# Building a neighbourhood bias in single transfers across the first feed-forward block

## Chip, cores and metric

One core of a Trainium2 chip. The time is device microseconds of one execution; three runs of the kernel before are known.

## What is computed

The reference is a small transformer trunk in float32 on 256 tokens (a grid of 4 rows by 64 columns) and 16 meta tokens, width 1024. Layer 0 mixes tokens by neighbourhood attention, layer 1 by differential attention, and each layer has a SwiGLU feed-forward block (FFN, hidden width 2816) before and after the mixing:

```python
for i in range(DEPTH):                                     # DEPTH = 2
    g = norm_g[i]
    f1 = swiglu(rmsnorm(h, g[0]), ffn_w_gate[i, 0], ffn_w_up[i, 0], ffn_w_down[i, 0])
    h = h + FFN_RES * rmsnorm(f1, g[1])
    hn = rmsnorm(h, g[2])
    if i % N_MIXERS == 0:
        m = neighborhood_attention(hn, ..., na_rpb[j], na_meta_bias[j])
    else:
        m = diff_attention(hn, ..., t5_rel_bias, lambda_init)
    h = h + rmsnorm(m, g[3])
    f2 = swiglu(rmsnorm(h, g[4]), ffn_w_gate[i, 1], ffn_w_up[i, 1], ffn_w_down[i, 1])
    h = h + FFN_RES * rmsnorm(f2, g[5])
```

In the neighbourhood attention each of 16 heads adds to a logit a learned bias that depends on the offset between query and key (`rpb`, 16 x 15 x 31), and a query sees only 16 columns of keys. The change is about how that bias, with the mask of the columns, is put together on the chip.

## The kernel before

**Weights.** All weights stream from DRAM as 328 units of 128 x 8 x 128 floats (512 KB) in the order of their use. `load` (line 110) issues one transfer from SyncE (SP) into one of 5 `raw` buffers. ScalarE writes the rounded half `whi` (line 126, `split_hi`) and VectorE the rest `wlo` (line 132, `split_lo`), two operations each, into one of 7 split slots (`W_BUFS`). A product is three matmuls, `mm3` (lines 179 to 181): whi with the data's high part, wlo with the high part, whi with the low part. A unit has 24 of them. The end of a unit's split frees its raw buffer, and `split_lo` then issues the next load; so the load of unit i + 5 stands on SP behind the split of unit i. A split needs a free slot, that is the last product of the unit seven before.

**The first FFN** (`ffn`, line 420). Its up part has 22 steps f. A step is two units (gate and up, 48 matmuls), then `evac(f)`: VectorE scales both sums (lines 436, 437), ScalarE takes the Silu, and VectorE multiplies and stores the result in two parts. Inside `evac` two further units are split. Steps 0 to 2 are set up by `start`; from f=3 on, one function of the list `extra` is called after each `evac`. Then come the down products, 22 units in 8 output tiles m, with a split per unit (`pump`) for 16 of 22 positions and `post.feed` after each tile.

**The bias** (`natten_bias`, line 559) is that list `extra`. In order: `small_loads`, `begin`, nothing, four `expand`, nothing, eight `mask`; 16 steps, so f=3 to f=18. `begin` loads the mask (128 x 2 x 160) and issues four transfers DRAM to DRAM, which cut the padded table `rpbP` into four copies `tab`, in pieces of 4 floats (line 570). `expand(rq)` issues two transfers that spread table rq over 32 partitions, 16 heads by 160 floats each (line 579). `mask` adds the mask to 4 heads at once (line 586), and POOL copies the meta bias in (line 590). All transfers are issued by SP, in program order, on one queue; SP waits at a load until the split that frees its buffer is done, and what is behind waits too.

**Order.** Within an engine the order is that of the code. PE's order is written out by hand (`manual_schedule`). The bias is first read by the neighbourhood attention (line 746).

Of the kernel before, what the change touches and what calls it, by code (L numbers as in the profile page):

```python
# [17 lines left out]
P = 128  # L18
# [8 lines left out]
ROWS = 4  # L27
# [20 lines left out]
def encoder_kernel(ctx, tc, xT, wall, gT, bqkvT, boT, sublnT, rpbP, metab, lam_p, rel,  # L48
# [23 lines left out]
    def acc_tile():  # L72
        """a bank for sums; outside attention its banks are taken too"""
        pools["turn"] = (pools["turn"] + 1) % 7
        if pools["wide"] and pools["turn"] % 2:
            return att_tile()
        return psum.tile([P, 512], F32, tag="acc", name=nm("acc"), bufs=4)
# [6 lines left out]

# [1 line left out]
    h = state.tile([P, KB, T], F32, tag="h", name="h")  # L86
# [14 lines left out]

# [1 line left out]
    # the split of unit i takes the slot of unit i - W_BUFS, so it comes after that one's  # L103
    # last product in the engines' order
    raw = {}
# [33 lines left out]
    def split_part(k, nk):  # L139
        """parts of the first units' splits"""  # L140
        for ahead in range(FIRST):
            split_hi(k, nk, ahead)
        for ahead in range(FIRST):
            split_lo(k, nk, ahead if k + nk < KB else 0)

    def pump_hi():
        """the first half of a split's work, if there is a slot; pump_lo does the rest"""
        i = count["split"]
        pending[0] = i < UNITS and i - W_BUFS < count["done"]
        if pending[0]:  # L150
            split_hi(0)
            split_hi(KB // 2)
# [30 lines left out]
    def proj(acc, n, ihi, ilo, hook=None):  # L183
        """products of one unit"""
        w = next_unit()
        for k in range(KB):
            if hook is not None and k in hook:
                hook[k]()
            mm3(acc[:, :n], w[0][:, k, :], w[1][:, k, :], ihi[:, k, :n], ilo[:, k, :n], k == 0, k == KB - 1)
        done()  # L190

    def proj_group(units, n_of, ihi, ilo, accs, hook):
        """k-outer products of several units, each into its own bank"""
        ws = [next_unit() for _ in units]
# [11 lines left out]

# [1 line left out]
    first = [load((2, 2, 4)) for _ in range(FIRST)]  # L208
# [23 lines left out]

# [1 line left out]
    def chunks(n):  # L234
        """first tokens of chunks of 128 that cover n tokens"""
        return (0, P, T - P) if n == T else (0, P)

    def sums_of(st, col, sq, n):
        """sums over the partitions of sq, with tokens on partitions"""
        cs = chunks(n)  # L240
        for i, c in enumerate(cs):
            nc.tensor.matmul(st[:, col + i:col + i + 1], sq[:, c:c + P], ones, start=True, stop=True)
        return st[:, col:col + len(cs)]
# [16 lines left out]
    def spread(st, r, n):  # L260
        """the tokens' values on all partitions, in PSUM"""
        for i, c in enumerate(chunks(n)):
# [20 lines left out]
    class InputRstd:  # L283
        """the token's 1/rms of h, computed between products"""

# [21 lines left out]
    class Post:  # L307
        """post-norm of one sub-layer, fed tile by tile: h grows by r * f with f the
        fed tiles times their gain and r the token's 1/rms"""

# [52 lines left out]
    def enter(post, n_of, ab, rest):  # L363
        """the first products of a sub-layer. Those of its first unit begin before the
        last post-norm is known: with h = h' + r f they are W h' + r (W f). Those of the
        units after it are k-outer, as h comes."""
        n0 = n_of(0)
# [28 lines left out]

# [1 line left out]
    def start(n):  # L398
        """the first products of all, as the data come"""
        gain = gains(0, 0)  # L400
# [19 lines left out]
    def ffn(l, which, n, before, gain_next, n_next, extra=()):  # L420
        extra = list(extra)
        with all_banks(), tc.manual_schedule():
# [6 lines left out]
            with tc.tile_pool(name=nm("ffn"), bufs=1) as fp:  # L429
# [17 lines left out]
                with tc.tile_pool(name=nm("fft"), bufs=2) as ft:  # L447
# [10 lines left out]
                    if which == 0:  # L458
                        nc.scalar.activation(warm, ones, AF.Exp)
                        if l == 1:  # L460
                            lambda_scalar()
                assert not extra
                if gain_next is None:
# [6 lines left out]
                for m in range(KB):  # L470
                    ps = acc_tile()
                    for f in range(FT):
                        idx = m * FT + f
                        if idx % KB == 0:
                            if w is not None:
                                done()
                            w = next_unit()
                            if idx % FT < 16:
                                pump(1)
# [3 lines left out]
                    if m < KB - 1:  # L483
                        for i in range(m + m // 6, m + 1 + (m + 1) // 6):
                            input_hi(i, gain_next, n_next)
                            input_lo(i, gain_next, n_next)
                done()
            return post

    def last_down(lp, mhi, mlo):  # L490
        """the last products, with tokens on partitions, and the last post-norm"""
        f = fg.rearrange("p a b -> p (a b)")[:, :2 * D].rearrange("p (t d) -> p t d", t=2)
# [18 lines left out]
        def finish(t, c):  # L511
            """statistics and gain of one piece"""
            at, n = pieces[t][c]
# [43 lines left out]

# [1 line left out]
    def natten_bias(holder):  # L559
        """steps that build the logit bias of the neighbourhood attention"""  # L560
        steps = []
        holder["tab"] = dram.tile([H0, ROWS, 79, ROWS], F32, tag="tab0", name="tab0")

        def begin():
            bt = biasp.tile([P, H0 * 2 * NK], F32, tag="bias", name="bias0")
            holder["b0"] = bt.rearrange("p (h q k) -> p h q k", h=H0, q=2)
            holder["wm"] = pools["tmp"].tile([P, 2, 160], F32, tag="wmask", name="wm", bufs=1)
            nc.sync.dma_start(holder["wm"], wmask)
            for rq in range(ROWS):
                nc.sync.dma_start(holder["tab"][:, rq, :, :], rpbP[:, :, 7 - rq:11 - rq])  # L570

        def expand(rq):
            def go():
                for qt in range(2):
                    src = holder["tab"][:, rq, :, :].rearrange("h x r -> h (x r)")
                    src = bass.AP(src.tensor, src.offset + (0 if qt == 0 else 32),
                                  [[4, 32], [ROWS * 79 * 4, H0], [1, 160]])
                    o = 0 if qt == 0 else NMETA
                    nc.sync.dma_start(holder["b0"][rq * 32:(rq + 1) * 32, :, qt, o:o + 160], src)
            return go  # L580

        def mask(qt, h0):
            def go():
                b4, wm = holder["b0"], holder["wm"]
                o = 0 if qt == 0 else NMETA
                nc.vector.tensor_tensor(out=b4[:, h0:h0 + 4, qt, o:o + 160], in0=b4[:, h0:h0 + 4, qt, o:o + 160],
                                        in1=wm[:, qt, :].unsqueeze(1).broadcast_to([P, 4, 160]), op=ALU.add)
                o = 160 if qt == 0 else 0
# [3 lines left out]

        return ([small_loads, begin, lambda: None] + [expand(r) for r in range(ROWS)] + [lambda: None]
                + [mask(qt, h0) for qt in range(2) for h0 in range(0, H0, 4)])

    tab1 = dram.tile([H1, T5N], F32, tag="tab1", name="tab1")

    def t5_bias(holder):
        """steps that build the relative-position bias of the differential attention"""
        nst = T5N // T5CH + 1  # L600
# [68 lines left out]
    def grid_rev(ap):  # L669
        """[p, (c r)] -> [p, q, c', r] with the columns from last to first"""  # L670
        return ap.rearrange("p (c r) -> p c r", r=ROWS)[:, ::-1, :].rearrange("p (q c) r -> p q c r", q=2)

    def q_order(ap):
        """[p, (q r c')] -> [p, q, c', r]"""
        return ap.rearrange("p (q r c) -> p q c r", q=2, r=ROWS)
# [4 lines left out]
    def token_order(ap):  # L680
        """[p, (q r c')], last tile first, -> [p, q, c, r]"""
        return ap[:, :NG].rearrange("p (q r c) -> p q c r", q=2, r=ROWS)[:, :, ::-1, :]

# [1 line left out]
    def natten(l, b4, before, gain_next, n_next):  # L685
        with ExitStack() as outer, ExitStack() as inner:
# [117 lines left out]

            # meta queries against meta keys, some pairs of heads at once
            meta = {}
# [64 lines left out]
    class Filler:  # L871
        """products that need no attention, to be set between its steps"""

# [34 lines left out]
    def pipeline(fl, steps, pumps, single=()):  # L908
        """attention of the pairs of heads, with products in between: a pair begins every
        8 chunks, and steps are (chunk from the pair's beginning, function of the pair)"""  # L910
        steps = sorted(steps, key=lambda t: -t[0])
# [31 lines left out]

# [1 line left out]
    def diff_attention(l, b4, before, gain_next, n_next):  # L945
# [139 lines left out]

# [1 line left out]

# [10 lines left out]
def _units(inputs):  # L1098
    """weights as [units, 128, 8, 128] in the order of their use"""
    def cols(w):  # L1100
# [28 lines left out]
def _t5_bucket(rel):  # L1129
    """bucket of a relative position: halves by sign, exact below 8, then by thresholds"""  # L1130
    n = np.abs(rel)
# [5 lines left out]
def _constants():  # L1137
# [7 lines left out]

    wm = np.zeros((P, 2, 160), np.float32)
    cq = np.arange(P) % 32
    kc = np.arange(160) // 4
    for qt, (c, k) in enumerate(((63 - cq, kc + 24), (31 - cq, kc))):
# [39 lines left out]
```

## Time and profile before

| | |
|---|---|
| Three runs | 1108.76, 1117.27, 1122.29 us (median 1117.27) |
| Span of the profiled execution | 1120.7 us (its time outside the span isn't given) |
| PE busy | 1093.9 us, 98% |
| VectorE (DVE) busy | 777.2 us, 69% |
| ScalarE (ACT) busy | 611.7 us, 55% |
| Weight loads | 326 of 512 KB, 3.9 us to landing (median) |
| Table transfers | 4 of 19.8 KB, 14.6 us to landing |
| Bias transfers | 8 of 320 KB, 19.2 us to landing |

A slice of the page is 1/40 of the span, 28 us. The shares are means over stages: what a stage costs is seen in windows of it and in the chain of waits, which follows the work that ended last back through what released it. Matmuls are pipelined: each is shown with 0.29 us, but they start 0.126 us apart.

### The profile page before, as it was taken

To read this page: it belongs to the slowest core of one execution; us is meant where nothing else is said; L and a number is where in the kernel's file an instruction comes from. 1 tells how busy PE (TensorE), PEld (TensorE's weight loads), DVE (VectorE), ACT (ScalarE), POOL (GpSimd) and SP (SyncE) were. 2 spreads that over 40 slices of the span, in tenths; PEclk is the share of its full clock that TensorE was granted. 3 is DMA by queue.
4 is the path that set the end of the run, shared out by engine and by line. 5 is a ranking of instruction groups with operands and counts; after the bars stand their busy time and mean duration, and the time that the engine had idled before them with its cause. 6 is when DMAs were issued, how large, how long until landed. Compare 5 with 4: busy or idle time off the path is not lost.

```text
span 1120.7 us, 22216 instructions
## 1 busy us (share of the span) xinstructions
PE 1093.9 (98%) x8492; PEld 1060.0 (95%) x8492; DVE 777.2 (69%) x1645; ACT 611.7 (55%) x1398; POOL 131.8 (12%) x234
## 2 busy tenths in 40 slices
PE   7988899999999999999999999999999999999997
PEld 7988899999989999999999999999989999999986
DVE  5745696578677796666568766566886778966643
ACT  4533456548667464445545544455577865655541
POOL 4000000043122300000011000001311222000000
PEclk9998999999999999999999999999999999999999
DMA  7569866525333275496534655465253242755551
GB/s 248 175 95 206 214 209 211 183 96 182 101 113 107 84 230 187 161 225 213 178 124 134 224 171 169 161 207 183 75 167 118 95 151 83 242 187 187 189 169 38
DMA packets 64955, 181.90 MB, mean 162 GB/s; under 512 B 13832, under 2 KB 22192, under 8 KB 64848
## 3 DMA queue, kind: packets, MB, share of 16 engines
q1 hardware_dynamic: 64848, 180.48, 53.4%
q8 instruction: 67, 1.10, 0.4%
q14 instruction: 40, 0.33, 0.1%
HBM read 179.33 MB, written 1.20 MB: 161 GB/s over the span
## 4 chain that ended last, share of the span: by engine, by line
PE 82%; DVE 8%; DMA 5%; issue 2%; ACT 2%; POOL 0%; SPq 0%; POOLq 0%; DVEq 0%; ACTq 0%
PE acc L179 14%; PE acc L181 14%; PE acc L180 14%; PE att L179 9%; PE att L181 8%; PE att L180 8%; DVE wlo L132 3%; DMA raw<-wall 3%; DMA bias<-tab 2%; DVE h L357 1%; DVE xlo L280 1%; ACT whi L126 1%; PE acc L200 1%; PE acc L204 1%; PE acc L509 1%
## 5 line engine op out<-in xcount | busy, mean ns | idle before, releaser
L132 DVE TENSOR_TENSOR wlo<-raw,whi 128x512 fp32r<-128x512 f32 (+1 forms) x660 | 438.5, 703 | 83.3 <-ACT whi L126 79.6
L126 ACT CAST whi<-raw 128x512 fp32r<-128x512 f32 (+1 forms) x660 | 374.1, 612 | 122.0 <-issue 43.3
L179 PE MATMUL acc<-xhi,whi 128*128 128x272 f32 (+1 forms) x1016 | 300.5, 296 | 5.6 <-ACT whi L126 5.6
L180 PE MATMUL acc<-xhi,wlo 128*128 128x272 f32 (+1 forms) x1016 | 292.8, 288 | 0.7 <-DVE wlo L132 0.7
L181 PE MATMUL acc<-xlo,whi 128*128 128x272 f32 (+1 forms) x1016 | 293.1, 288 | 0.0
L179 PEld LDWEIGHTS acc<-xhi,whi 128*128 128x128 f32 x1016 | 192.6, 190 | 11.7 <-ACT whi L126 6.0
L180 PEld LDWEIGHTS acc<-xhi,wlo 128*128 128x128 f32 x1016 | 192.8, 190 | 1.3 <-DVE wlo L132 1.3
L181 PEld LDWEIGHTS acc<-xlo,whi 128*128 128x128 f32 x1016 | 192.7, 190 | 0.0
L179 PE MATMUL att<-xhi,whi 128*128 128x272 f32 (+1 forms) x560 | 161.9, 289 | 4.6 <-ACT whi L126 4.6
L180 PE MATMUL att<-xhi,wlo 128*128 128x272 f32 (+1 forms) x560 | 161.3, 288 | 0.7 <-DVE wlo L132 0.7
L181 PE MATMUL att<-xlo,whi 128*128 128x272 f32 (+1 forms) x560 | 161.5, 288 | 0.0
L438 ACT ACTIVATE gt<-gt 128x272 f32<-128x272 f32 (+1 forms) x88 | 37.7, 428 | 152.7 <-DVE gt L436 152.7
L179 PEld LDWEIGHTS att<-xhi,whi 128*128 128x128 f32 x560 | 106.2, 190 | 5.7 <-ACT whi L126 5.0
L180 PEld LDWEIGHTS att<-xhi,wlo 128*128 128x128 f32 x560 | 106.1, 189 | 1.1 <-DVE wlo L132 1.1
L181 PEld LDWEIGHTS att<-xlo,whi 128*128 128x128 f32 x560 | 106.2, 190 | 0.0
L179 PE MATMUL acc<-mhi,whi 128*128 128x272 f32 x286 | 83.0, 290 | 0.0
L181 PE MATMUL acc<-mlo,whi 128*128 128x272 f32 x286 | 82.5, 289 | 0.0
L180 PE MATMUL acc<-mhi,wlo 128*128 128x272 f32 x286 | 82.4, 288 | 0.0
L273 POOL TENSOR_TENSOR sqa<-sqa,sq 128x272 f32<-128x272 f32 (+1 forms) x66 | 55.6, 843 | 167.9 <-ACT sq L268 164.9
L179 PE MATMUL att<-mhi,whi 128*128 128x272 f32 x242 | 70.2, 290 | 0.0
L181 PE MATMUL att<-mlo,whi 128*128 128x272 f32 x242 | 69.8, 289 | 0.0
L180 PE MATMUL att<-mhi,wlo 128*128 128x272 f32 x242 | 69.7, 288 | 0.0
(248 smaller groups left out, 1959.1 us busy)
## 6 DMA issues: line engine op xcount, KB each, us to landing
raw<-wall SPq DMA_DIRECT2D x326, 512.0 KB, 3.9
bias<-tab SPq DMA_DIRECT2D x8, 320.0 KB, 19.2
bias<-tab SPq DMA_DIRECT2D x8, 256.0 KB
h<-xT SPq DMA_DIRECT2D x3, 272.0 KB, 5.2
out<-ht SPq DMA_DIRECT2D x3, 256.0 KB
raw<-wall SPq DMA_DIRECT2D x4, 128.0 KB, 3.2
raw<-wall SPq DMA_DIRECT2D x2, 256.0 KB
grow<-glast SPq DMA_DIRECT2D x1, 512.0 KB, 5.0
```

The source lines that it names most:

```text
L126: nc.scalar.copy(split[i][0][:, sl], raw[i][:, sl])
L132: nc.vector.tensor_tensor(out=wlo[:, sl], in0=raw[i][:, sl], in1=whi[:, sl].bitcast(F32), op=ALU.subtract)
L179: nc.tensor.matmul(ps, whi_k, mhi, start=first, stop=False)
L180: nc.tensor.matmul(ps, wlo_k, mhi, start=False, stop=False)
L181: nc.tensor.matmul(ps, whi_k, mlo, start=False, stop=last)
L200: nc.tensor.matmul(accs[j][:, :n], ws[j][0][:, k, :], ihi[:, k, :n], start=k == 0, stop=False)
L204: nc.tensor.matmul(accs[j][:, :n], ws[j][0][:, k, :], ilo[:, k, :n], start=False, stop=k == KB - 1)
L273: nc.gpsimd.tensor_tensor(out=t[:, :n], in0=acc[:, :n], in1=sq[:, :n], op=ALU.add)
L280: nc.vector.scalar_tensor_tensor(out=xlo[:, m, :n], in0=h[:, m, :n], scalar=gain[:, m:m + 1], in1=xhi[:, m, :n].bitcast(F32), op0=ALU.mult ...
L357: nc.vector.tensor_tensor(out=h[:, m, :n], in0=h[:, m, :n], in1=fg[:, m, :n], op=ALU.add)
L438: nc.scalar.activation(gt[:, :n], gt[:, :n], AF.Silu)
L509: nc.tensor.matmul(o, b, whi, start=False, stop=last)
```

## The change

`begin` issues only the mask. The four table transfers become steps of their own, `table(r)`, at f=5 to 8. `expand` is called for one `rq` and one `qt`, so it issues one transfer, and an empty step stands ahead of each: they go out after f=10, 12, 14, 16, 18 and 20 and, since the list is now longer than the up part, at units 0 and 2 of the down products. The down loop takes one step per unit. The eight mask steps follow two empty ones and fall on units 5 to 12. The mask has one value per key column (128 x 2 x 40) and is added head by head, the value repeated over the 4 rows. The buffer of the mask moves to a pool that stays open. The removal of comments in the diff is left out here.

```diff
 # ffn
-                assert not extra
                 if gain_next is None:
...
                             w = next_unit()
+                            if extra:
+                                extra.pop(0)()
                             if idx % FT < 16:
                                 pump(1)
...
+                assert not extra
                 done()

 # natten_bias
-            holder["wm"] = pools["tmp"].tile([P, 2, 160], F32, tag="wmask", name="wm", bufs=1)
+            holder["wm"] = biasp.tile([P, 2, 40], F32, tag="wmask", name="wm")
             nc.sync.dma_start(holder["wm"], wmask)
-            for rq in range(ROWS):
-                nc.sync.dma_start(holder["tab"][:, rq, :, :], rpbP[:, :, 7 - rq:11 - rq])
-
-        def expand(rq):
+
+        def table(rq):
+            return lambda: nc.sync.dma_start(holder["tab"][:, rq, :, :], rpbP[:, :, 7 - rq:11 - rq])
+
+        def expand(rq, qt):
             def go():
-                for qt in range(2):
-                    src = holder["tab"][:, rq, :, :].rearrange("h x r -> h (x r)")
-                    src = bass.AP(src.tensor, src.offset + (0 if qt == 0 else 32),
-                                  [[4, 32], [ROWS * 79 * 4, H0], [1, 160]])
-                    o = 0 if qt == 0 else NMETA
-                    nc.sync.dma_start(holder["b0"][rq * 32:(rq + 1) * 32, :, qt, o:o + 160], src)
+                src = holder["tab"][:, rq, :, :].rearrange("h x r -> h (x r)")
+                src = bass.AP(src.tensor, src.offset + (0 if qt == 0 else 32),
+                              [[4, 32], [ROWS * 79 * 4, H0], [1, 160]])
+                o = 0 if qt == 0 else NMETA
+                nc.sync.dma_start(holder["b0"][rq * 32:(rq + 1) * 32, :, qt, o:o + 160], src)
             return go
...
-                nc.vector.tensor_tensor(out=b4[:, h0:h0 + 4, qt, o:o + 160], in0=b4[:, h0:h0 + 4, qt, o:o + 160],
-                                        in1=wm[:, qt, :].unsqueeze(1).broadcast_to([P, 4, 160]), op=ALU.add)
+                for hd in range(h0, h0 + 4):
+                    b = b4[:, hd, qt, o:o + 160].rearrange("p (c r) -> p c r", r=ROWS)
+                    nc.vector.tensor_tensor(out=b, in0=b, in1=wm[:, qt, :].unsqueeze(2).broadcast_to([P, 40, ROWS]),
+                                            op=ALU.add)
...
-        return ([small_loads, begin, lambda: None] + [expand(r) for r in range(ROWS)] + [lambda: None]
-                + [mask(qt, h0) for qt in range(2) for h0 in range(0, H0, 4)])
+        steps = [small_loads, begin] + [table(r) for r in range(ROWS)]
+        for r in range(ROWS):
+            for qt in range(2):
+                steps += [idle, expand(r, qt)]
+        return steps + [idle] * 2 + [mask(qt, h0) for qt in range(2) for h0 in range(0, H0, 4)]
```

SP's queue from the loads of step f=4 on, before (`raw` are weight loads, `tab` the tables, `bias` the expanded bias; numbers tell buffers apart):

```order
L116 DMA raw_632<-wall 128x1024
L116 DMA raw_642<-wall 128x1024
L568 DMA wm<-wmask 128x320
L570 DMA tab_124<-rpbP 16x79x4 x4
L116 DMA raw_713<-wall 128x1024
L116 DMA raw_723<-wall 128x1024
L116 DMA raw_787<-wall 128x1024
L116 DMA raw_797<-wall 128x1024
L579 DMA bias_644<-tab_124 32x16x160 x2
L116 DMA raw_863<-wall 128x1024
L116 DMA raw_873<-wall 128x1024
L579 DMA bias_644<-tab_124 32x16x160 x2
```

The same place after the change:

```order
L116 DMA raw_632<-wall 128x1024
L116 DMA raw_642<-wall 128x1024
L570 DMA wm<-wmask 128x80
L116 DMA raw_709<-wall 128x1024
L116 DMA raw_719<-wall 128x1024
L573 DMA tab_124<-rpbP 16x79x4
L116 DMA raw_784<-wall 128x1024
L116 DMA raw_794<-wall 128x1024
L573 DMA tab_124<-rpbP 16x79x4
L116 DMA raw_859<-wall 128x1024
L116 DMA raw_869<-wall 128x1024
L573 DMA tab_124<-rpbP 16x79x4
```

Two weight loads now stand ahead of each table. The bias transfers, further on in the queue, stand singly with four loads between them:

```order
L116 DMA raw_1083<-wall 128x1024
L116 DMA raw_1093<-wall 128x1024
L581 DMA bias_644<-tab_124 32x16x160
L116 DMA raw_1158<-wall 128x1024
L116 DMA raw_1168<-wall 128x1024
L116 DMA raw_1232<-wall 128x1024
L116 DMA raw_1242<-wall 128x1024
L581 DMA bias_644<-tab_124 32x16x160
```

In before two of them stood together, with two loads between the pairs. VectorE in the down products after the change (`wlo` are splits, `fg` and `flo` belong to `post.feed`):

```order
L132 TENSOR_TENSOR wlo_2054<-raw_1903,whi_2053 128x512 x2
L593 TENSOR_TENSOR bias_644<-bias_644,wm 128x160 x4
L328 TENSOR_SCALAR fg<-att_2014,gh_sb 128x272
L132 TENSOR_TENSOR wlo_2103<-raw_1913,whi_2102 128x512 x2
L338 SCALAR_TENSOR_TENSOR flo_1921<-fg,g_sb,fhi_1920 128x272
L280 SCALAR_TENSOR_TENSOR xlo<-h,g_sb,xhi 128x272
L593 TENSOR_TENSOR bias_644<-bias_644,wm 128x160 x4
L132 TENSOR_TENSOR wlo_2137<-raw_1954,whi_2136 128x512 x2
```

The masks stand between splits of the down products, four operations at a time; before, one operation stood behind each `evac` from f=11 to f=18.

## Rows read from the trace of the kernel before

**Rows 1.** The page's 40 slices: PE busy, granted PE clock (tenths), GB/s.
```profile
PE   7988899999999999999999999999999999999997
PEclk9998999999999999999999999999999999999999
GB/s 248 175 95 206 214 209 211 183 96 182 101 113 107 84 230 187 161 225 213 178 124 134 224 171 169 161 207 183 75 167 118 95 151 83 242 187 187 189 169 38
```
**Rows 2.** Windows, PE: stretch, its length, busy us (matmuls), clock, DMA share, GB/s.
```profile
28.00:78.00 50.00, 50.00 (x400) 1.00 0.56 129
78.00:128.00 50.00, 38.49 (x258) 0.90 1.04 205
128.00:178.00 50.00, 50.00 (x398) 1.00 0.68 220
```
**Rows 3.** Chain that ended last, 60 to 130 us: start, us, what.
```profile
66.50 15.80 DMA raw<-wall
...
84.35 14.41 DMA raw<-wall
...
102.04 20.00 DMA bias<-tab
```
**Rows 4.** Timeline of SP: start, us of issuing, line, transfer.
```profile
58.49 7.91 SPq L570 DMA_DIRECT2D tab<-rpbP  x4
66.50 6.44 SPq L116 DMA_DIRECT2D raw<-wall  x4
```
**Rows 5.** One line's transfers and landing: first table; weight loads, 130 to 200 us.
```profile
L570 SPq DMA_DIRECT2D tab<-rpbP x1: 653/653/653, 58.5 to 58.5; - x1
...
DMA to landing us min/median/max: 11.8/11.8/11.8
...
L116 SPq DMA_DIRECT2D raw<-wall x28: 327/328/328, 130.6 to 196.9; - x28
...
DMA to landing us min/median/max: 3.2/3.4/4.6
```
**Rows 6.** Timeline of PE, then of VectorE: start, us, operation, idle before.
```profile
79.86 0.29 PE L181 MATMUL acc<-xlo,whi 128*128 128x272 f32 x1
83.05 0.39 PE L179 MATMUL att<-xhi,whi 128*128 128x272 f32 x1 [2.90 <-ACT whi L126]
...
59.02 1.29 DVE L132 TENSOR_TENSOR wlo<-raw,whi 128x512 fp32r<-128x512 f32 x2
60.59 1.29 DVE L132 TENSOR_TENSOR wlo<-raw,whi 128x512 fp32r<-128x512 f32 x2
...
68.77 0.43 DVE L443 TENSOR_TENSOR mlo<-ut,mhi 128x272 fp32r<-128x272 f32 x1
...
122.06 0.82 DVE L586 TENSOR_TENSOR bias<-bias,wm 128x640 f32<-128x640 f32 x1 [3.35 <-DMA bias<-tab]
```
**Rows 7.** The page's DMA issues: count, size of one, median us to landing.
```profile
raw<-wall SPq DMA_DIRECT2D x326, 512.0 KB, 3.9
bias<-tab SPq DMA_DIRECT2D x8, 320.0 KB, 19.2
```
**Rows 8.** Windows of all engines; PE, PEld, DVE, ACT, POOL, clock, DMA, GB/s.
```profile
61.00:66.00 5.00, 5.00 (x42) 5.00 (x42) 4.72 (x10) 2.83 (x6) 0.00 (x0) 1.00 0.53 40
66.00:72.00 6.00, 6.00 (x50) 6.00 (x49) 2.93 (x7) 1.78 (x4) 0.00 (x0) 1.00 0.28 5
72.00:81.00 9.00, 8.15 (x65) 7.93 (x63) 0.00 (x0) 0.00 (x0) 0.00 (x0) 1.00 0.78 47
81.00:85.00 4.00, 1.62 (x6) 1.42 (x7) 1.97 (x4) 1.37 (x3) 0.00 (x0) 0.83 0.97 338
85.00:123.00 38.00, 31.38 (x212) 30.30 (x210) 16.48 (x33) 11.68 (x24) 0.00 (x0) 0.88 1.12 201
```
**Rows 9.** The tile bias: instructions, ns min/median/max, first and last start.
```profile
L746 DVE CUSTOM_DVE_ANT_0 L<-att,bias x32: 288/336/343, 258.1 to 341.8; 128x176 f32<-128x176 f32 x32
...
L579 SPq DMA_DIRECT2D bias<-tab x8: 431/1876/3721, 73.0 to 103.5; - x8
```
**Rows 10.** Window of all engines, as rows 8, in the down products.
```profile
190.00:210.00 20.00, 20.00 (x161) 20.00 (x160) 12.62 (x22) 10.51 (x21) 2.35 (x3) 1.00 0.48 150
```

## What I predict, and why

> **What bounds the kernel now.** I began with the page's slices: TensorE (PE) is busy nearly everywhere, but the slices between about 56 and 140 us show 8s and the only PEclk digit of 8, while the transfer rate falls to 95 GB/s [rows 1]. So the kernel is bound by PE, and this stage, the up products of the first FFN, is where PE isn't fed. PE's own stretches say how much that costs: 400 and 398 products in the 50 us on either side, 258 in 78 to 128 us [rows 2]. At 50/399 = 0.1253 us a product, the 141 missing ones are 17.7 us. [...]
>
> The chain of waits names what PE was short of: 15.8 and 14.4 us in weight loads, then 20.0 us in a bias transfer [rows 3]. SP's timeline shows why the loads were late. Four table transfers are issued together, which takes 7.91 us, and the load behind them goes out at 66.50 [rows 4]. It lands at 66.50 + 15.80 = 82.3; undisturbed loads land 3.4 us after issue [rows 5]. PE's last product before the gap starts at 79.86, the next at 83.05, 0.75 us after that landing [rows 3, 6]. I call that load's unit 22: the loop evac asked for it in its step f=5.
>
> **What a transfer costs the queue.** All go through one queue, so I price each in queue time.
> - A weight unit is 512 KB [rows 7]. At the best stretch's 338 GB/s that is 1.55 us, at the 248 GB/s of the first slice 2.1 us [rows 1, 8]; I take 1.9, as the loads here rarely run alone.
> - A table moves 79x16 pieces of 16 bytes. From 61 to 81 us the rate is 40, 5 and 47 GB/s, and at 81 it is back at 338 [rows 8]. In those 20 us four tables and some 0.8 of a weight unit (9 us at 47 GB/s) passed: (20 - 1.5)/4 = 4.6, without that deduction 5.0 us. I take 4.8. The low end is nothing, and then the margin below only grows; the high end is the first table's own landing, 11.8 us [rows 5].
> - A bias transfer is 320 KB [rows 7]. From 85 to 123 us, 201 GB/s for 38 us [rows 8] is 7.64 MB; eight of these are 2.62 MB, the rest 9.6 weight units, 18.2 us: (38 - 18.2)/8 = 2.5 us each. By the bytes alone, at 338 GB/s, it would be 1.0; by its landing in the crowd 19.2 [rows 7]. The 2.5 is used because it already contains the crowd.
>
> [...]
>
> **The change, part by part.**
> *Tables one per step.* Nothing is removed from the queue: the same four tables, now with two weight loads ahead of each, at f=5 to 8. In before each step brings two loads as well, but SP issued all four tables first. A step of PE is 48 x 0.1253 = 6.0 us; the queue's is 4.8 + 2 x 1.9 = 8.6. So the queue loses 2.6 us in each of four steps, and the question is whether the cover holds. The splits of units 17 and 18 end at 59.02 + 1.29 and 60.59 + 1.29, that is 60.3 and 61.9 [rows 6]; that frees the slots for units 22 and 23, which are now issued at once, before the first table. From 62.2 the queue works without a pause through unit 23, then table, two units, three times over, then the fourth table and unit 30: eight units and four tables, 15.2 + 19.2 = 34.4 us, to 96.6. With 3.4 - 1.9 = 1.5 us to land and 0.75 to the first product, unit 30 is ready at 98.9. PE without a gap wants unit 22 at 80.0, unit 30 eight units of 3.0 us later, at 104.0. The margin is 5.2 us, the smallest of the stage (unit 28, a table earlier, has more). It is used up when a table costs 4.8 + 5.2/4 = 6.1 us.
>
> *Bias transfers singly, every second step.* Two steps of PE are 12.0 us; four units and one bias transfer take 7.6 + 2.5 = 10.1. The queue gains 1.9 us at each, so the margin grows from there. In before the eight sat in four steps: 2 x 2.5 + 3.8 = 8.8 us against 6.0, right behind the tables, when the cover was gone. SP's issues themselves (0.4 to 3.7 us a transfer when the queue is full [rows 9]) move with them, and only weight loads stand behind them.
>
> *Masks during the down products.* Before: eight operations of 640 values, 0.82 us each [rows 6]. After: 32 of 160. From 640 values in 0.82 and 272 in 0.43 us, a value is 1.06 ns and an operation 0.14 us, so 160 values take 0.31 and four 1.25 us; if the repeated mask value made each as slow as a 272-wide one, 1.7. That is 10 to 14 us instead of 6.6. VectorE is busy 12.62 of 20 us there [rows 10], so eight units (24 us) have 8.9 us to spare: it falls 1 to 5 us behind the splits, which are up to seven units, 21 us, ahead of PE. Price on the path: nothing; without that cover, those 1 to 5 us. The first mask operation also waits for the last bias transfer, issued three units (9 us) before. Should that land after 19.2 us as in the crowd, VectorE waits 10 us, with splits queued behind it: still inside 21. The first reader of the bias starts at 258.1 [rows 9], some 50 us after the last mask. The two POOL copies of the meta bias move along, and a smaller mask (40 columns) saves 80 KB of transfer: both nothing.
>
> [...]
>
> **Sum.** 1120.7 - 17.7 = 1103.0 us of span. What lies around the span isn't shown; the slowest run, 1122.3, is 1.6 above, so I add 1: **1104 us**. The profile is 3.4 us above the median of the three runs, and they lie 13.5 us apart; that spread would come from this stage too, and a kernel without the pauses would lie below all three.
>
> **Rivals.**
> [...]
> [...]
> [...]
>
> **Chances.** Forecast (1100 to 1107) 0.72, part stays (1107 to 1113) 0.15, nothing gained 0.06, slower 0.05, better than 1100 0.02. The range 1099 to 1112 takes the first and most of the second. 2% is about what a measurement of this kernel can tell from no change: that is below 1095 or above 1140. Only a loss in before that I haven't seen gives the first, and I leave it the 0.02 of that case; only the dear end of the last rival gives the second, 0.03, which leaves 0.95 for within 2%.
>
> **What would show it.** In the profile after: no PE gap and clock 1.00 from 56 to 140 us, about 399 products in each 50 us; each table followed by two weight loads that land within about 10 us, and single bias transfers; masks of 0.3 us among the down products with VectorE never late. Wrong would be: a PE gap near the units loaded at f=7 and 8 (table price over 6.1), or one in the down products (masks).

## The result: 1104.2 us, and the same time in every run

The changed kernel takes 1104.22 us (median of 6 runs, 1104.07 to 1104.48). The kernel before has a median of 1114.75 us over six runs, the three known ones among them (1108.76 to 1122.29). The ratio is 0.9891, 95% interval 0.9864 to 0.9918: about 10.5 us or 1.1% less. That is under the 2% which the prediction takes for the least that can be told, yet the interval keeps clear of 1. The profiled execution has a span of 1102.4 us. Two single runs of about 2689 us, one of the kernel before and one without the bias, are slow ones and count in no number below.

The page's slices of the changed kernel (PE busy and granted clock in tenths, then GB/s) show no 8 on PE between 56 and 140 us any more (the 8 of the first slice lies ahead of this stage):

```profile
PE   8999999999999999999999999999999999999997
...
PEclk8999999999999999999999999999999999999999
...
GB/s 252 178 151 212 275 228 168 176 73 182 110 97 135 110 224 172 178 239 192 175 69 210 192 185 164 181 184 172 77 173 96 111 140 113 241 184 185 184 167 39
```

PE's windows of 50 us, columns as in [rows 2], have 399 products in each of the three; before, the middle one had 258:

```profile
28.00:78.00 50.00, 50.00 (x399) 1.00 0.70 172
78.00:128.00 50.00, 50.00 (x399) 1.00 1.04 225
128.00:178.00 50.00, 50.00 (x399) 1.00 0.77 220
```

The chain of waits from 56 to 140 us consists of products alone, where [rows 3] had 15.8, 14.4 and 20.0 us of transfers. SP's timeline (start, us of issuing) shows the new order: two weight loads, a table, and later four loads, a bias transfer. The four loads behind the last table take SP 13.75 us; PE doesn't notice.

```profile
60.72 1.89 SPq L116 DMA_DIRECT2D raw<-wall  x2
62.65 0.65 SPq L573 DMA_DIRECT2D tab<-rpbP  x1
64.99 1.88 SPq L116 DMA_DIRECT2D raw<-wall  x2
66.92 0.55 SPq L573 DMA_DIRECT2D tab<-rpbP  x1
69.26 3.80 SPq L116 DMA_DIRECT2D raw<-wall  x2
73.11 0.54 SPq L573 DMA_DIRECT2D tab<-rpbP  x1
73.75 3.27 SPq L116 DMA_DIRECT2D raw<-wall  x2
77.07 4.03 SPq L573 DMA_DIRECT2D tab<-rpbP  x1
81.22 13.75 SPq L116 DMA_DIRECT2D raw<-wall  x4
95.02 0.73 SPq L581 DMA_DIRECT2D bias<-tab  x1
97.35 8.15 SPq L116 DMA_DIRECT2D raw<-wall  x4
105.55 1.41 SPq L581 DMA_DIRECT2D bias<-tab  x1
```

How much cover was left is read from two rows. The first half of unit 30's split starts on ScalarE at 98.93, after a wait for its load; PE comes to that unit at 104.03:

```profile
98.93 1.14 ACT L126 CAST whi<-raw 128x512 fp32r<-128x512 f32 x2 [2.09 <-DMA raw<-wall]
```
```profile
104.03 0.29 PE L179 MATMUL acc<-xhi,whi 128*128 128x272 f32 x1
```

In the kernel before, such a split began at 82.38, and PE's product came 0.67 us later, at 83.05 [rows 6]:

```profile
82.38 1.14 ACT L126 CAST whi<-raw 128x512 fp32r<-128x512 f32 x2 [14.01 <-DMA raw<-wall]
```

By the same 0.67 us unit 30 was ready at 99.6, 4.4 us before it was wanted.

### The profile page after: what moved, and what is told of

The parts are those of the page before. It is cut to its first block, busy times and chain, and to the rows that moved or that the text cites. A ratio compares the mean times of both kernels' runs of the same rounds, so it can differ in the third digit from the quotient of the medians.

```text
span 1102.4 us, 22240 instructions
## 1 busy us (share of the span) xinstructions
PE 1089.8 (99%) x8492; PEld 1057.4 (96%) x8492; DVE 779.9 (71%) x1669; ACT 612.6 (56%) x1398; POOL 131.9 (12%) x234
## 4 chain that ended last, share of the span: by engine, by line
PE 90%; DVE 6%; issue 2%; ACT 1%; POOL 0%; DMA 0%; SPq 0%; POOLq 0%; DVEq 0%; ACTq 0%
PE acc L179 16%; PE acc L181 15%; PE acc L180 15%; PE att L179 10%; PE att L181 9%; PE att L180 9%; DVE xlo L280 1%; DVE wlo L132 1%; DVE h L357 1%; PE acc L200 1%; PE acc L204 1%; PE acc L509 1%; PE acc L511 1%; PE acc L510 1%; PE acc L201 1%
```

## Experiments

The theory: each transfer costs time in one queue, and PE pauses only where the debt exceeds the cover of units already loaded and split. Rivals: the tables in a row are the whole loss; the bias pairs are the whole loss; a table alone is as dear as 11.8 us; the masks or something else of the bias is still on the path.

### Only the tables apart

The kernel before with this edit; the bias transfers stay in pairs, now at f=9 to 12, and the masks in the up part, now at f=14 to 21:

```diff
-            for rq in range(ROWS):
-                nc.sync.dma_start(holder["tab"][:, rq, :, :], rpbP[:, :, 7 - rq:11 - rq])
+        def table(rq):
+            return lambda: nc.sync.dma_start(holder["tab"][:, rq, :, :], rpbP[:, :, 7 - rq:11 - rq])
...
-        return ([small_loads, begin, lambda: None] + [expand(r) for r in range(ROWS)] + [lambda: None]
+        return ([small_loads, begin] + [table(r) for r in range(ROWS)] + [expand(r) for r in range(ROWS)] + [lambda: None]
```

> The kernel before, but its four tables are issued one per step at f=5 to 8 as in the changed kernel; the eight bias transfers stay in pairs, now at f=9 to 12 right behind the tables, and the masks stay in the up part. Theory of the queue (each transfer costs queue time, and PE pauses once the debt is larger than the cover): about 5 us of cover are left after the tables, then four steps of 8.8 us of queue against 6.0 us of PE make 11 us of debt, so some 6 us idle and 2 at the lower clock: 1112 us, between 1109 and 1115, with the pause at units loaded behind the last bias pairs. If the tables put together are the whole loss: 1104. If the bias pairs are the whole loss: 1115, as before.

Measured: 1114.29 us against 1115.35 of the kernel before on the same chip; ratio 0.9988, 0.9962 to 1.0013. This half of the change alone gains nothing that can be measured. The last products ahead of PE's first two pauses now start at 115.9 and 124.5 us instead of 79.9 (rows of its timeline behind the pauses; in brackets the idle time ahead of the row and what ended it):

```profile
117.88 0.39 PE L179 MATMUL att<-xhi,whi 128*128 128x272 f32 x1 [1.70 <-ACT whi L126]
...
127.53 0.39 PE L179 MATMUL att<-xhi,whi 128*128 128x272 f32 x1 [2.73 <-ACT whi L126]
```

The tables were covered, and the bias pairs behind them then used up what was left: the pauses stand at units loaded behind the second and third pair (loads issued at 99.17 and 108.44) and not, as expected, behind the last. By its time alone this run fits the rival as well by which the pairs are the whole loss (1115); the next one excludes that. The chain of this run, from 60 us on, shows weight loads and, at its end, a bias transfer for which the masks wait.

```profile
64.24 27.15 DMA raw<-wall x2
...
93.97 14.40 DMA raw<-wall
...
113.18 17.04 DMA bias<-tab
```

### Only the bias transfers apart

The changed kernel with the four tables together again. Its masks stay in the down products, since each of them needs the transfers of all four `rq`; so this half of the change is the single transfers and the later masks, which aren't tested apart:

```diff
             nc.sync.dma_start(holder["wm"], wmask)
+            for rq in range(ROWS):
+                nc.sync.dma_start(holder["tab"][:, rq, :, :], rpbP[:, :, 7 - rq:11 - rq])
...
-        steps = [small_loads, begin] + [table(r) for r in range(ROWS)]
+        steps = [small_loads, begin] + [idle] * ROWS
```

> The changed kernel, but the four tables are issued together at f=4 as before; bias transfers stay single, every second step, and the masks stay in the down products. Theory of the queue: the first pause of before stays (3.5 us idle and 1.6 at the lower clock, at the unit loaded behind the tables), and with single bias transfers, which gain 1.9 us every two steps, none comes after it: 1109 us, between 1107 and 1111. If the tables put together are the whole loss: 1115, as before. If the bias pairs are: 1104.

Measured: 1110.83 us (1109.44 to 1112.23), ratio 0.9959, 0.9940 to 0.9978. One pause is left, at the unit loaded behind the tables, and none after it:

```profile
84.30 0.39 PE L179 MATMUL att<-xhi,whi 128*128 128x272 f32 x1 [4.04 <-ACT whi L126]
```
```profile
78.00:128.00 50.00, 45.62 (x347) 0.97 0.91 259
128.00:178.00 50.00, 50.00 (x399) 1.00 0.76 212
```

The 52 products short of 399 are 6.5 us at 0.1253, and 1104.2 + 6.5 = 1110.7. So the halves give 1.1 and 4.5 us alone. The changed kernel itself wasn't run beside them; against its 1104.22 the two together give 11.1. They draw on one cover, and neither is the whole loss.

The masks had a part in the loss of before that the theory of the queue leaves out. VectorE sat idle for 3.35 us ahead of the first mask, which waited for a bias transfer [rows 6]. The sums of that step stood behind it, then ScalarE's Silu, then the next split, and PE paused for that split:

```profile
123.33 0.43 ACT L438 ACTIVATE gt<-gt 128x272 f32<-128x272 f32 x1 [5.42 <-DVE gt L436]
```
```profile
124.32 0.39 PE L179 MATMUL att<-xhi,whi 128*128 128x272 f32 x1 [1.67 <-ACT whi L126]
```

With 0.34 us more at the next product, this fourth pause is 2.0 of the 11.5 us idle in that window (50 - 38.49 [rows 2]). Whether its load would have been late anyway isn't shown.

### One, two and four tables more

The changed kernel with spare tables, each written to a DRAM tensor of its own that nothing reads, behind the fourth table, behind the third and fourth, or behind all four (the diff is that with four; the others have `(3,)` and `(2, 3)`):

```diff
+        spare = {rq: dram.tile([H0, 79, ROWS], F32, tag=f"spare{rq}", name=f"spare{rq}") for rq in (0, 1, 2, 3)}
+
         def table(rq):
-            return lambda: nc.sync.dma_start(holder["tab"][:, rq, :, :], rpbP[:, :, 7 - rq:11 - rq])
+            def go():
+                nc.sync.dma_start(holder["tab"][:, rq, :, :], rpbP[:, :, 7 - rq:11 - rq])
+                if rq in spare:
+                    nc.sync.dma_start(spare[rq], rpbP[:, :, 7 - rq:11 - rq])
+            return go
```

> The changed kernel with one more table transfer, of the same shape into a spare DRAM tensor that nothing reads, right behind the fourth table (f=8). Queue theory: 4.8 us more of queue against the 4.4 us by which the first half of unit 30 was ready early in the changed kernel: 1104 to 1106, a pause of 0 to 1 us at units 30 to 32. If a single table holds the queue for 11.8 us, a pause of 7 us and 2 at the lower clock: 1113.

> The changed kernel with one spare table transfer behind each of the third and fourth tables (f=7 and 8). Queue theory: 9.6 us more of queue against 4.4 of margin, so about 5 us idle and 2 at the lower clock, in one or two pauses: 1111 us, between 1108 and 1113. At 11.8 us a table: 19 idle, 1127.

> The changed kernel with one spare table transfer behind each of the four tables. Queue theory: 19.2 us more of queue against 4.4 of margin, 15 us idle and 4 to 6 at the lower clock: 1124 us, between 1119 and 1128, and from two extra tables to four 9 to 13 us more. At 11.8 us a table: 43 idle, over 1145. If spread tables mostly hide behind loads: under 1110.

Measured: 1104.47, 1105.86 (1104.81 to 1108.16) and 1115.42 us (1113.71 to 1117.04). One more table is covered, as expected; with two the loss begins, but at 1.6 us instead of 7; with four it is 11.2 instead of 20. Both lie outside the ranges that I had expected. The shape is that of a debt against a cover, and 11.8 us a table is excluded, but a table more costs less than 4.8 us. ScalarE's rows for unit 30, with one, two and four extra, say how much:

```profile
103.27 1.14 ACT L126 CAST whi<-raw 128x512 fp32r<-128x512 f32 x2 [6.81 <-DMA raw<-wall]
```
```profile
103.96 1.14 ACT L126 CAST whi<-raw 128x512 fp32r<-128x512 f32 x2 [7.26 <-DMA raw<-wall]
```
```profile
110.91 1.14 ACT L126 CAST whi<-raw 128x512 fp32r<-128x512 f32 x2 [6.73 <-DMA raw<-wall]
```

Against 98.93 the unit is 4.3, 5.0 and 12.0 us later. So the extra table behind the fourth adds 4.3 us, that behind the third only 0.7 more, and those behind the first two 3.5 each. Single figures are good to about 1 us: unit 28 is 1.3 us earlier with one extra table than in the changed kernel, though nothing ahead of it differs. Why the price changes with the place wasn't tried. With four extra, the window of 78 to 128 us shows what the pauses cost beyond idle time:

```profile
78.00:128.00 50.00, 44.66 (x314) 0.90 0.87 168
```

5.3 us are idle, but 85 products are missing, 10.7 us: half of the loss is the lower clock after the pauses (mean granted 0.90, so 5 of the 50 us).

### The masks twice, and not at all

```diff
-                for hd in range(h0, h0 + 4):
+                for hd in 2 * list(range(h0, h0 + 4)):
```

> The changed kernel with each of the 32 mask operations done twice (the masked logits stay far below all others). My theory prices the masks at nothing, as the splits are up to 21 us ahead of PE: 1104.2 us within 0.5, with some 10 us more of VectorE work between the down products. If the masks were on the path, up to 10 us more: 1114.

Measured: 1104.06 us (1103.96 to 1104.45). VectorE's busy time (third engine column) in the 24 us of the masks goes up, and PE has 193 products in both; first the changed kernel, then the masks twice:

```profile
164.00:188.00 24.00, 24.00 (x193) 24.00 (x192) 20.89 (x53) 12.44 (x24) 2.97 (x4) 1.00 0.48 158
```
```profile
164.00:188.00 24.00, 24.00 (x193) 24.00 (x192) 23.41 (x70) 11.66 (x24) 8.29 (x4) 1.00 0.42 136
```

In the reverse, `range(h0, h0 + 4)` became `range(0)`:

> The changed kernel without the 32 mask operations (that part of the computation is left out); tables and bias transfers stay. If the 2.1 us belong to VectorE's work or to waits between the masks and the down products: 1102. Since doing the masks twice cost nothing, my theory says 1104.2 within 0.5, and the 2.1 us then belong to the transfers.

1103.81 us (1103.60 to 1103.92), 0.4 less than the changed kernel, which wasn't run beside it. The masks are covered where they stand now.

### No bias building, and the tables given

One kernel builds nothing (the step list ends after `begin`, which sets the bias to zero); one gets the tables as an input, laid out ahead of the launch:

```diff
-            nc.sync.dma_start(holder["wm"], wmask)
+            nc.gpsimd.memset(bt, 0.0)
...
-        return steps + [idle] * 2 + [mask(qt, h0) for qt in range(2) for h0 in range(0, H0, 4)]
+        return [small_loads, begin]
```
```diff
-        holder["tab"] = dram.tile([H0, ROWS, 79, ROWS], F32, tag="tab0", name="tab0")
+        holder["tab"] = rpbP
...
-            return lambda: nc.sync.dma_start(holder["tab"][:, rq, :, :], rpbP[:, :, 7 - rq:11 - rq])
+            return lambda: None
...
```

> The changed kernel without the building of the neighbourhood bias: no mask transfer, tables, bias transfers or mask operations; the bias is set to zero once (this part of the computation is left out). My theory: nothing of it is on the path any more, so 1104.2 us within 0.5. If a part of it still costs, through slower loads or VectorE, the time falls by that part, below 1103.

> The same kernel as the one without any building of the bias (the bias is zero, that part of the computation is left out), for an undisturbed profile. 1102.0 us again. If the 2.1 us lie in the first FFN, PE reaches the attention 2 us earlier than in the changed kernel; if not, the stage after it, or the ends of the program, show it.

> The changed kernel with the four tables laid out ahead of the launch and given as an input; the bias transfers read from it, and the four table transfers are gone. Theory of the queue: the tables are hidden already, so 1104.2 us within 0.5, and the cover behind f=8 is larger by up to 19 us. If the 2.1 us that the kernel without any bias building gained over the changed kernel belong to the tables: 1102.

Without the bias: 1102.01 and, in a second set of runs, 1101.75 us. That is 2.2 to 2.5 us below the changed kernel, where I expected nothing. But they don't lie in the first FFN. Counted by products, PE is 0.19 us earlier than in the changed kernel at product 100 (22.8 us) and still 0.19 earlier at product 1800 (237 us), behind the whole stage. At the last product it is 1.79 us earlier. Most of that comes at three places where later sub-layers meet: 0.43 us at 369, 0.25 at 768 and 0.66 at 920; some 0.7 us of the span lie outside PE's products. The 0.25 at 768 is no effect of the bias: the kernel with the masks twice, which builds all of it, has the same step. The other two places show no such step in the runs that build the bias. There PE waits for a sum of squares from POOL, 0.3 and 0.6 us, and without the bias it doesn't. PE's waits on it over the whole span (us, times, longest), in the changed kernel and then without the bias:

```profile
PE st L242 <- POOL sqa L273: 1.7, 4, 0.6
```
```profile
PE st L242 <- POOL sqa L273: 0.8, 2, 0.5
```

With the tables given the time is 1103.76 us (1103.41 to 1103.95), 0.5 less, but counted by products PE isn't earlier anywhere behind the first 25 us. So nothing of the bias is on the path in this stage. Why two of the places behind it are shorter without it stays open; the engines' orders are the same but for the steps left out and the zeroing on POOL.

What the four tables cost the queue can be read from the run with the tables given. Its split of unit 30 (the same place in ScalarE's order) starts 11.2 us earlier than the 98.93 of the changed kernel, and it waits for no load:

```profile
87.71 1.14 ACT L126 CAST whi<-raw 128x512 fp32r<-128x512 f32 x2
```

## Why the prediction was right, step by step

- **What bounds the stage** held. The 141 missing products were to come back and did: 399 in the window. Of the 17.7 us that they stand for, 11.5 were idle time (50 - 38.49 [rows 2]); the other 6.2 fell into a window whose granted clock was 0.90 on average. The 1.6 to 2 us at the lower clock behind a pause, in what I expected of the runs, was my estimate; with the tables together it was 6.5 - 4.4 = 2.1. The span fell from 1120.7 to 1102.4, 18.3 us; I had 17.7. That the profile of before was a slow example was also said, though by some 5 us and not 3.4, since a span is less than its time; against the median the gain is 10.5 us. The spread of before came with the pauses, as supposed: with them 13.5 us, without them 0.4.
- **Tables one per step.** Unit 30 was to be ready at 98.9 with 5.2 us to spare, and was at 99.6 with 4.4; PE wanted it at 104.03 for a predicted 104.0. That the sum is good to 0.7 us is in part luck, for two terms of it were off and nearly cancel. With the tables given, the split at 87.71 makes unit 30 ready at 88.4; the sum without its four tables, 98.9 - 19.2, has it ready at 79.7. So the loads took 8.7 us more than a queue "without a pause": the loads at 64.99 and 69.26 wait on SP for VectorE's splits, which end at 64.96 and 69.23. And the four tables made the unit 11.2 us later and not 19.2, that is 2.8 each where I had 4.8. (Their time in the queue may be longer than this delay, since without them the splits wait for no load.) I had the 4.8 from four tables in a row; that it holds for a table between loads was my estimate, and no run shows it. Nor was unit 28 clearly better off: its split begins at 92.67, so it is ready at 93.3 and wanted at 97.97, 4.6 us to spare. So the break-even of 6.1 us a table can't be carried elsewhere. The 4.8 is the step that failed in what I expected of two and four extra, where a table cost 0.7 to 4.3.
- **Bias transfers singly.** They land in 9.9 us (median) instead of 19.2 [rows 7]. They go out at 95.02, 105.55, 114.99 and 123.84: 10.5, 9.4 and 8.9 us for two steps, where PE needs 12.0. I had 10.1 for the queue. That this half of the change, and not the tables, prevents the later pauses is shown by the first two experiments together: with the pairs kept, PE pauses behind them though the tables stand apart; with single transfers nothing follows the pause of the tables. What the later masks add to it isn't shown apart.
- **Masks.** An operation takes 0.315 us (0.31 expected); four take 1.02 from the first's start, since they overlap, so I had 1.25 too high. VectorE had 3.1 us left in the 24 us of the masks, where I had it 1 to 5 us behind. The many small operations cost nothing here: twice the number didn't move the time (1104.06 us against 1104.22). A slip without weight: the mask's transfer fell from 160 to 40 KB, by 120 and not by 80.
- **The rivals.** A table that holds the queue for 11.8 us is excluded: one spare table cost 4.3. That a part of the pause stays, the case with 0.15, was closer than it looks: two extra tables, which made unit 30 ready 5.0 us later, are enough to begin it.
- **The signs.** PE without a gap, clock 1.00, 399 products and masks of 0.3 us came true. One didn't: loads behind a table were to land within about 10 us, and those behind the later three whose landing the trace shows took 12.5, 18.5 and 14.5. PE didn't pause for them, with the 4.4 us that were left.
- **Around the span** lie 1.8 us (1104.21 against 1102.4) where I added 1; this and the 0.6 by which the span was lower nearly cancel.

## What to carry to other kernels

Price a transfer in time of the queue, put the debt of a stretch against the cover of what is already loaded, and find the one unit where the margin is smallest. Where several bursts share a cover, spreading one of them may show nothing, as the tables alone did (1114.29 us against 1115.35), until the other is spread too. A kernel whose runs differ by 1% while another's agree within 0.04% may well have such a debt just above its cover.

## What the runs showed of the hardware that I had not expected

- A table of 16-byte pieces slowed the loads behind it. After the first one the queue moved 70 GB/s for 8 us, though the next two transfers on SP were weight loads and the second table's 16-byte packets start only at 74.3; then it moved 151 for 22 us (windows of the changed kernel; clock, DMA share, GB/s):

```profile
62.00:65.00 3.00, 1.00 0.84 253
65.00:73.00 8.00, 1.00 0.86 70
73.00:95.00 22.00, 1.00 1.07 151
95.00:99.00 4.00, 1.00 1.00 207
```

  The same 8 us with the tables given:

```profile
65.00:73.00 8.00, 1.00 0.79 256
```

  The DMA share is no lower with the table than without it: the engines count as busy while a packet takes longer. One of 4 KB took 0.75 us there on average, and 0.20 with the tables given.
- The pauses cost one and a half times to twice their idle time. With four extra tables 5.3 us of idle made 10.7 us of missing products; with the tables together 4.4 made 6.5; before, 11.5 made 17.7. Not every pause was followed by a lower clock: of the four of before, the first three are followed by a granted clock of 0.50, the last, 2.0 us, by 1.00 (stretches of 2.5 to 3 us close behind each, from 83.8, 108.0, 118.5 and 125.3).
- In the changed kernel's profile PE's granted clock is 0.88 over the first 28 us, and no time is lost by it. Against two runs at 1.00 there, product 100 is 0.19 us late (without the bias) and 0.30 early (tables given). PE was idle for 3.2 us of the first 20 at the lower clock and for 5.5 and 6.0 at the full one, so these products wait for something else anyway.
